# Spatial gating finished in two rounds, expert matrices stored by tile, and the last rows fetched right behind the last adds, in an encoder layer on one Trainium2 core

## The chip, the core and the metric

The kernel runs on 1 core of one Trainium2 chip. The metric is the device time of one execution in microseconds (us); smaller is better. The engines are TensorE (PE, matrix products), VectorE (DVE), ScalarE (ACT), GpSimd (POOL, which also issues the indirect DMAs) and SyncE (SP, which issues all other DMAs).

## What is computed

One layer (T = 2048 tokens, D = 1024) in float32: an input projection to q, k, v, u and vs (512 columns each), neighbourhood attention on q, k, v, spatial gating on u and vs, an output projection with a layer norm, and a mixture of 16 SwiGLU experts (width 256) of which each token takes two of one group, with a second layer norm. What matters here, cut from the reference:

```python
def spatial_gating(u, vs, ln_g, ln_b, w_s, b_s):          # u, vs after gelu
    vg = vs.reshape(B, T, 8, 64)
    vg = layer_norm(vg, ln_g.reshape(8, 64), ln_b.reshape(8, 64))
    vg = vg.reshape(B, n_chunks, 128, 8, 64)
    mixed = jnp.einsum('gpq,bnqgd->bnpgd', w_s, vg) + jnp.transpose(b_s)[:, :, None]
    return u * mixed.reshape(B, T, 512)

for e in range(16):
    act = jax.nn.silu(hf @ w_gate[e]) * (hf @ w_up[e])
    y = y + combine[:, e:e + 1] * (act @ w_down[e])
x = layer_norm(DEEPNORM_ALPHA * x + y, ln2_g, ln2_b)
```

## The kernel before

Each float32 product is made of three passes: both operands are split into a high part (a cast on ACT, line 142) and a low part (a subtraction on DVE, line 143), and PE adds high by high, low by high and high by low (lines 132 to 134).

*Phase A* is the input projection. The tokens go in two halves; `block(h, col, ...)` multiplies half `h` by column group `col` (0 q, 1 k, 2 v, 3 u, 4 vs) in two sets of four units, each in 8 k-steps. The order is (0,2), (0,4), (0,1), (0,3), (0,0), (1,0), (1,4), (1,3), (1,1). What follows a set is a generator (`fin_vs` for column group 4, `fin_k` for 1, `fin_u` for 3): after each k-step's matmuls the `Pipe` runs every live generator up to its next `yield`, and the order in which they issue is the order on every engine. For each set of column group 4 `fin_vs` takes a gelu and sums (lines 246, 247), subtracts the means and squares piece by piece (lines 251, 254, 255), raises the variance to −1/2 on POOL (line 259), multiplies (line 265), applies gain `gb` and offset `bb` on POOL (lines 267, 268), splits into `vh` and `vl`, and multiplies by the 8 position matrices `wsh`, `wsl` into PSUM tile `mx` (2 buffers). The result plus the bias `bs` goes to tile `mt` (lines 288, 290) and from there to DRAM (`md`, line 294), where `fin_u` fetches it. `mt` has one buffer; `fin_k` uses the same room for two of the four pieces that it stores to `kd` (line 343, function `rooms`).

*The experts* are jobs j = 0 to 17, each with four quarters u = 0 to 3 (gate and up of two column tiles; `gate_up`), then `down(j)`, one job later. `load_gu` (lines 1058, 1060) fetches one 1024 x 128 matrix tile from `w_gate` or `w_up`, and `load_d` (line 1082) half a down matrix; each is split on ACT and DVE unless the job is 17. `gather` (line 1112) brings token rows, `flip` (line 1131) transposes them, the scaled result `y` (line 1206) is added to `xad` in DRAM by an indirect DMA (line 1227). All indirect DMAs stand in POOL's queue.

The tokens are in four groups of experts. When a group's experts are done, `combine` fetches each tile of its rows (`fetch`, line 1449), waits `WAIT` steps, normalises it (`stats` on DVE, lines 1423, 1425; POOL, lines 1426, 1431; `first` and `second` on DVE, lines 1435, 1438) and stores it (`place`, line 1456). From job 15 on `CT` says at which quarters the next tile starts. The last group is done by `last`, whose table `TAIL` sets the order: `f` fetch, `s` statistics on DVE, `a` statistics on ACT (`act_stats`, lines 1473 to 1479), `c` and `v` the two DVE passes, `d` the last expert's product added to a fetched row (lines 1195, 1495), `o` store. The first entry of the table is issued at job 17, quarter 2.

Of the kernel before, what the change touches and what calls it, by code (L numbers as in the profile page):

```python
# [17 lines left out]
P = 128  # L18
# [22 lines left out]
NVT = 12  # L41
PSTART = 21
LATE = 14
YA = 3
YB = 2
YG = 0
FIRST = 256
WARM = 8
# [11 lines left out]
D32 = (17,)  # L60
DN = 0, 0
TU = 3
CT = (0, 2)
TAIL = "f0 f3 f1 f4 f2", "s0 c0 d3 a1 v0 d4 o0 c1 a2 v1 o1 c2 a3 v2 o2 a4 c3 v3 o3 c4 v4 o4"
AW1 = 3
AW2 = 4
LW = (1, 2), (2, 1)
# [78 lines left out]
def phase_a(c, xT, w_in, wsT, bsT, sg_g, sg_b):  # L146
# [8 lines left out]
    with ExitStack() as es:  # L155
# [54 lines left out]
        def load_sgu():  # L210
            nt, ng = 3 * E * S // P, 8 * T // P
            z = sp.tile([P, nt + ng], I32, name="mt")
            zt, zg = z[:, 0:nt].rearrange("p (r o) -> p r o", o=3), z[:, nt:].rearrange("p (r o) -> p r o", o=2)
            nc.vector.memset(z, 0)
            for v in (zt, zg):
                nc.vector.memset(v[:, :, 1:2], NONE)
            nc.vector.memset(zg[:, :, 0:1], T)
            nc.sync.dma_start(c.table[:, :].rearrange("(p c) o -> p c o", p=P), zt)
            nc.sync.dma_start(c.gtok[:, :].rearrange("(p c) o -> p c o", p=P), zg)
            nc.sync.dma_start(gb, bcast(sg_g, 512))  # L220
            nc.sync.dma_start(bb, bcast(sg_b, 512))
            nc.sync.dma_start(bs, bsT)
            wsr = sp.tile([P, 8, P], F32, name="mt")
            nc.sync.dma_start(wsr, wsT)
            yield
            yield
            split(nc, wsh[:, :, :], wsl[:, :, :], wsr[:, :, :])
            yield pipe

        def fin_v(h, units, ps):  # L230
# [10 lines left out]
        def fin_vs(h, units, ps):  # L241
            q = (h * 8 + units[0]) // 4
            g = [ev.tile([P, 8, 64], F32, name="g", bufs=8) for _ in range(4)]
            su = ev.tile([P, 4, 8], F32, name="su")
            for n in range(4):
                nc.scalar.activation(g[n], ps[n], AF.Gelu_apprx_tanh)
                nc.vector.tensor_reduce(su[:, n], g[n], axis=AX.X, op=OP.add)
            yield
            va = ev.tile([P, 4, 8], F32, name="va")
            for n in range(4):  # L250
                nc.vector.scalar_tensor_tensor(g[n], su[:, n, :, None].to_broadcast([P, 8, 64]), -1.0 / 64, g[n],
                                               op0=OP.mult, op1=OP.add)
                sq = ev.tile([P, 8, 64], F32, name="sq")
                nc.scalar.activation(sq, g[n], AF.Square)
                nc.vector.tensor_reduce(va[:, n], sq, axis=AX.X, op=OP.add)
            nc.vector.tensor_scalar(va, va, 1.0 / 64, EPS, op0=OP.mult, op1=OP.add)  # L256
            yield
            r = ev.tile([P, 4, 8], F32, name="r")
            nc.gpsimd.tensor_tensor(r, va, mhalf[:, :, :], op=OP.pow)  # L259
            yield  # L260
            yield
            vh = sp.tile([P, 4, 512], F32R, name="vh")
            vl = sp.tile([P, 4, 512], F32R, name="vl")
            for n in range(4):
                nc.vector.tensor_tensor(g[n], g[n], r[:, n, :, None].to_broadcast([P, 8, 64]), op=OP.mult)
                f = g[n][:, :, :].rearrange("p a d -> p (a d)")
                nc.gpsimd.tensor_tensor(f, f, gb, op=OP.mult)
                nc.gpsimd.tensor_tensor(f, f, bb, op=OP.add)
                yield
            for _ in range(YA):  # L270
                yield
            for n in range(4):
                f = g[n][:, :, :].rearrange("p a d -> p (a d)")
                split(nc, vh[:, n, :], vl[:, n, :], f)
            for _ in range(YB):
                yield
            mt = sp.tile([P, 4, 512], F32, name="mt")
            for g2 in range(4):
                pm = mx.tile([P, 2, 4, 64], F32, name="mx")
                for j in range(2):  # L280
                    e = g2 * 2 + j
                    s = slice(e * 64, (e + 1) * 64)
                    passes(nc, pm[:, j], wsh[:, e, :], wsl[:, e, :], vh[:, :, s], vl[:, :, s], True, True)
                for j in range(2):
                    e = g2 * 2 + j
                    s = slice(e * 64, (e + 1) * 64)
                    if j:
                        nc.vector.tensor_scalar(mt[:, :, s], pm[:, j], bs[:, e:e + 1], None, op0=OP.add)
                    else:
                        nc.scalar.activation(mt[:, :, s], pm[:, j], AF.Identity, bias=bs[:, e:e + 1])  # L290
                if g2 % 2 or YG:
                    yield
            for n in range(4):
                nc.sync.dma_start(md[q * 4 + n], mt[:, n, :])
            yield pipe
# [688 lines left out]
class Moe:  # L984
# [56 lines left out]
    def load_gu(self, pipe, j, f, lag=1):  # L1041
# [7 lines left out]
            r = self.raw()[:, :].rearrange("p (k f) -> p k f", k=KC)  # L1049
            l = self.wp.tile([P, KC, P], F32R, name="wl")  # L1050
        m, q = divmod(f, 2)
        s = slice(m * P, (m + 1) * P)
        e = bass.ds(self.ex[pos], 1)
        if lo:
            r4 = r.rearrange("p (k o) f -> p k o f", o=2)
            for i in range(2):
                src = self.w[i][e, q * 512:(q + 1) * 512, s]
                nc.sync.dma_start(r4[:, :, i], src.rearrange("o (k p) f -> (o p) k f", p=P))
        else:
            self.issued = nc.sync.dma_start(r, self.w[q][e, :, s].rearrange("o (k p) f -> (o p) k f", p=P)).ins.name  # L1060
        self.gw[j, f] = (r, None) if whole else (h, l)
        if whole:
            return
# [222 lines left out]
    def main(self):  # L1286
# [150 lines left out]
        def second(z, r):  # L1437
            V.scalar_tensor_tensor(z, z, r, lnb[0:z.shape[0], :], op0=OP.mult, op1=OP.add)

        def norm(x):  # L1440
            mean, r = stats(x)
            first(x, x, mean, OP.subtract)
            yield
            second(x, r)
            yield
# [12 lines left out]
            tc.declare_no_dep(r.ins, group=group, reason="rows of other tokens")  # L1458
            tc.add_to_no_dep_group(group, r.ins)

        def combine(g, rec):
            x = fetch(g, rec)
            for _ in range(WAIT):
                yield
            yield from norm(x)
            place(x, rec)
            yield pipe

# [78 lines left out]
        def over(mi, i):  # L1547
# [5 lines left out]
            for q, w in enumerate((w_gate, w_up)):  # L1553
                t = self.xp[0].tile([P, KC, W], F32R, name=("xh", "xl")[q])
                f = t[:, :, 0:FF].bitcast(F32)
                nc.sync.dma_start(f, w[bass.ds(e, 1)].rearrange("o (k p) f -> (o p) k f", p=P))
                wts.append(f)
            wd = self.xp[1].tile([P, 2, D], F32, name="xh")
            nc.sync.dma_start(wd, w_down[bass.ds(e, 1)].rearrange("o (k p) d -> (o p) k d", p=P))
# [37 lines left out]
        for j in range(2, nj):  # L1597
# [4 lines left out]
            for u in range(4):  # L1602
# [24 lines left out]
                if j < nj - 1 and j - 1 in LASTS and u == (TU if j == nj - 4 else 3):  # L1627
                    todo += [(LASTS[j - 1], i) for i in range(GTILES[LASTS[j - 1]])]
                pipe.step()
                if todo and u in (CU if j < nj - 3 else CT):  # L1630
                    g, i = todo.pop(0)
                    pipe.add(combine(g, recs[g][:, i]))
                if j == nj - 1 and u >= 2:
                    if u == 2:
                        tail = last(GTILES[3])
                    else:
                        pipe.flush()
                        assert not todo
                    next(tail)
# [40 lines left out]
    return mid.transpose(1, 0, 2), edge  # L1680


# [32 lines left out]
```

## Time and profile before

| | |
|---|---|
| median of 3 runs | 1328.71 us (1328.42 to 1332.13) |
| the profiled execution | 1326.6 us |
| its span in the trace | 1324.9 us |
| PE busy | 1230.7 us, 93% of the span |
| DVE, ACT, POOL busy | 59%, 43%, 34% |
| mean granted clock of PE | 0.972 |
| moved by DMA | 261.73 MB, mean 198 GB/s |

The span is the time from the first to the last recorded instruction; the execution's own time is 1.7 us longer. PE's share of busy time is an average over stages with different limits, so the share alone does not say what a change in one stage is worth. The granted clock is the share of TensorE's full speed that the chip gave.

### The profile page before, as it was taken

How to read it: one execution, taken by the hardware profiler on the slowest of the kernel's cores; microseconds unless marked ns; L12 is line 12 of the kernel's file. 1: busy time of each engine (PE TensorE's matmuls, PEld its weight loads, DVE VectorE, ACT ScalarE, POOL GpSimd, SP SyncE). 2: the span in 40 equal slices, each digit the busy share in tenths (PEclk: the TensorE clock that was granted, in tenths of full speed). 3: DMA queues.
4: the chain of work that ended last, by engine and by line, in shares of the span. 5: the costliest groups of instructions: out<-in, count | busy, mean ns of one | idle time of the engine just before them, and what ended most of it. 6: DMA issues, size and time to landing. Idle time of an engine off the chain costs nothing. (4 is left out here: it accounts for less than half of the span.)

```text
span 1324.9 us, 22205 instructions
## 1 busy us (share of the span) xinstructions
PE 1230.7 (93%) x7932; PEld 1048.7 (79%) x7932; DVE 775.6 (59%) x1622; ACT 576.1 (43%) x1218; POOL 452.4 (34%) x448
## 2 busy tenths in 40 slices
PE   9998999999899997999999999988888999998980
PEld 7886888888788775888888888768777999998970
DVE  5358233424853226576676676876466568777655
ACT  5324233322342236545545445334466555555522
POOL 0046000003710013234435434442323357565475
PEclk9998999999899997999999999999999999999995
DMA  8602634450254689578668676372999999999984
GB/s 253 199 24 97 229 120 164 161 189 18 89 182 167 180 257 289 170 187 199 166 187 196 160 219 194 97 227 76 257 277 301 250 270 287 297 293 306 280 250 137
DMA packets 193506, 261.73 MB, mean 198 GB/s; under 512 B 51120, under 2 KB 126128, under 8 KB 193392
## 3 DMA queue, kind: packets, MB, share of 16 engines
q1 hardware_dynamic: 175408, 204.88, 51.6%
q0 software_dynamic: 17984, 55.40, 14.9%
q8 instruction: 63, 1.03, 0.3%
q14 instruction: 51, 0.42, 0.1%
HBM read 184.17 MB, written 80.24 MB: 200 GB/s over the span
## 5 line engine op out<-in xcount | busy, mean ns | idle before, releaser
L143 DVE TENSOR_TENSOR wl<-wr,wh 128x512 fp32r<-128x512 f32 (+1 forms) x132 | 139.4, 1063 | 96.8 <-ACT wh L142 95.6
L618 POOL TENSOR_SCALAR lg<-lg,s 128x352 f32<-128x352 f32 (+3 forms) x128 | 80.2, 626 | 289.6 <-DVE s L617 226.4
L142 ACT CAST wh<-wr 128x512 fp32r<-128x512 f32 (+1 forms) x132 | 109.6, 843 | 85.0 <-DMA wr<-w_in 41.1
L132 PE MATMUL acc<-wh,xh 128*128 128x512 f32 x320 | 125.9, 393 | 0.1
L133 PE MATMUL acc<-wl,xh 128*128 128x512 f32 x320 | 125.3, 392 | 0.2 <-DVE wl L143 0.2
L134 PE MATMUL acc<-wh,xl 128*128 128x512 f32 x320 | 125.3, 391 | 0.2
L132 PE MATMUL gu<-xh,wh 128*128 128x256 f32 (+2 forms) x416 | 124.5, 299 | 0.0
L134 PE MATMUL gu<-xh,wl 128*128 128x256 f32 (+2 forms) x416 | 124.0, 298 | 0.0
L133 PE MATMUL gu<-xl,wh 128*128 128x256 f32 (+2 forms) x416 | 123.9, 298 | 0.0
L132 PE MATMUL acc<-xh,wh 128*128 128x512 f32 x256 | 101.0, 395 | 0.7 <-DVE kt L143 0.7
L134 PE MATMUL acc<-xh,wl 128*128 128x512 f32 x256 | 100.3, 392 | 0.0
L133 PE MATMUL acc<-xl,wh 128*128 128x512 f32 x256 | 100.2, 391 | 0.0
L633 ACT COPY pT<-pt 128x384 f32<-128x384 f32 (+3 forms) x128 | 57.7, 451 | 97.4 <-PE pt L631 95.3
L605 DVE CUSTOM_DVE_ANT_0 lg<-l,tm 128x352 f32<-128x352 f32 (+3 forms) x128 | 57.8, 452 | 70.6 <-PE l L134 45.2
L259 POOL TENSOR_TENSOR r<-va,mhalf 128x32 f32<-128x32 f32 x4 | 22.5, 5636 | 212.3 <-DVE va L256 212.3
L1227 POOL DMA_INDIRECT xad<-y,ix x38 | 64.7, 1704 | 54.4 <-ACT y L1206 31.6
L1112 POOL DMA_INDIRECT xg<-x1d,ix x40 | 48.1, 1203 | 101.8 <-PE tp L1131 37.0
L132 PEld LDWEIGHTS gu<-xh,wh 128*128 128x128 f32 x416 | 79.5, 191 | 1.4
L133 PEld LDWEIGHTS gu<-xl,wh 128*128 128x128 f32 x416 | 79.2, 190 | 1.3
L134 PEld LDWEIGHTS gu<-xh,wl 128*128 128x128 f32 x416 | 79.1, 190 | 0.0
L134 PEld LDWEIGHTS acc<-wh,xl 128*128 128x128 f32 x320 | 60.3, 189 | 13.7 <-DVE xl L143 1.1
L133 PEld LDWEIGHTS acc<-wl,xh 128*128 128x128 f32 x320 | 60.4, 189 | 13.2 <-DVE wl L143 0.9
(325 smaller groups left out, 3230.2 us busy)
## 6 DMA issues: line engine op xcount, KB each, us to landing
wr<-w_in SPq DMA_DIRECT2D x72, 256.0 KB
wr<-w_down SPq DMA_DIRECT2D x34, 512.0 KB
kt<-kd SPq DMA_DIRECT2D x24, 704.0 KB
wr<-w_gate SPq DMA_DIRECT2D x30, 512.0 KB
wr<-w_up SPq DMA_DIRECT2D x30, 512.0 KB
sd<-kt SPq DMA_DIRECT2D x16, 512.0 KB
qb<-qd SPq DMA_DIRECT2D x64, 128.0 KB
sr<-sd SPq DMA_DIRECT2D x16, 512.0 KB
```

The lines of the kernel that those rows point to most:

```text
L132: nc.tensor.matmul(out, lhsT=ahi, rhs=bhi, start=first, stop=False)
L133: nc.tensor.matmul(out, lhsT=ahi, rhs=blo, start=False, stop=False)
L134: nc.tensor.matmul(out, lhsT=alo, rhs=bhi, start=False, stop=last)
L142: nc.scalar.copy(hi, src)
L143: nc.vector.tensor_tensor(lo, src, hi.bitcast(F32), op=OP.subtract)
L259: nc.gpsimd.tensor_tensor(r, va, mhalf[:, :, :], op=OP.pow)
L605: nc.vector.tensor_tensor_reduce(out=l[:, :N], in0=o.rearrange("p r c -> p (r c)"), in1=bias, scale=-1.0, scalar=3.0e38, op0=OP.add, op1=O ...
L618: nc.gpsimd.tensor_scalar(l[:, :N], l[:, :N], s, 1.0, op0=OP.mult, op1=OP.mult)
L633: nc.scalar.copy(w[0:n, 0:len(ch)], pt[0:n, 0:len(ch)])
L1112: nc.gpsimd.indirect_dma_start(out=self.xg[(self.slot[j] + s) % NXG][0:m, :], out_offset=None, in_=c.x1d[0:rows, :], in_offset=bass.Indire ...
L1227: return self.c.nc.gpsimd.indirect_dma_start(out=self.c.xad[0:rows, :], out_offset=bass.IndirectOffsetOnAxis(ap=ix, axis=0), in_=y, in_off ...
```

## The change

- *Gating.* In `fin_vs` the loop that subtracts and squares becomes two loops; the power is raised in the same step; the gain is applied on DVE before the power is needed; the offset goes out of the loop. Since the position product is linear, the offset's part of it is the row sum of each position matrix times the offset, which is computed once in `load_sgu` (8 one-column products, then `bb` becomes offset times row sum plus bias) and added by one DVE instruction per two matrices. All four pieces are split in one step, and the products come `YB` = 4 steps later (`YA` goes).
- *By tile.* `by_tile` lays `w_gate` and `w_up` out in memory, on the host, so that each 1024 x 128 tile has for each partition one run of 1024 floats (4 KB) where it had 8 runs of 128 (512 B).
- *The end.* Of the five tiles of group 2 (g = 2) the first starts at (14,3) as before, the others at (15,0), (15,1), (15,3) and (16,0) in place of (15,0), (15,2), (16,0) and (16,2); their statistics are taken on ACT, and one step sooner after the fetch. The first entry of `TAIL` is issued at quarter 1 of job 17, in the order f0 to f4; `TAIL` has no `s`.

```diff
@@ constants
-YA = 3
-YB = 2
+YB = 4
-CT = (0, 2)
-TAIL = "f0 f3 f1 f4 f2", "s0 c0 d3 a1 v0 d4 o0 c1 a2 v1 o1 c2 a3 v2 o2 a4 c3 v3 o3 c4 v4 o4"
+CT = (0, 1, 3), (0,)
+TAIL = "f0 f1 f2 f3 f4", "a0", "a1 c0 v0 o0 a2 c1 v1 o1 d3 a3 c2 v2 o2 d4 a4 c3 v3 o3 c4 v4 o4"
@@ load_sgu
             split(nc, wsh[:, :, :], wsl[:, :, :], wsr[:, :, :])
+            for _ in range(8):
+                yield
+            pr = mx.tile([P, 8], F32, name="mx")
+            for e in range(8):
+                nc.tensor.matmul(pr[:, e:e + 1], lhsT=wsr[:, e], rhs=c.ones, start=True, stop=True)
+            rs = sp.tile([P, 8], F32, name="rs")
+            nc.vector.tensor_copy(rs, pr)
+            for e in range(8):
+                s = slice(e * 64, (e + 1) * 64)
+                nc.vector.tensor_scalar(bb[:, s], bb[:, s], rs[:, e:e + 1], bs[:, e:e + 1], op0=OP.mult, op1=OP.add)
@@ fin_vs
+            for n in range(4):
                 sq = ev.tile([P, 8, 64], F32, name="sq")
                 nc.scalar.activation(sq, g[n], AF.Square)
...
-            yield
             r = ev.tile([P, 4, 8], F32, name="r")
             nc.gpsimd.tensor_tensor(r, va, mhalf[:, :, :], op=OP.pow)
+            yield
+            for n in range(4):
+                f = g[n][:, :, :].rearrange("p a d -> p (a d)")
+                nc.vector.tensor_tensor(f, f, gb, op=OP.mult)
+            yield
...
                 nc.vector.tensor_tensor(g[n], g[n], r[:, n, :, None].to_broadcast([P, 8, 64]), op=OP.mult)
                 f = g[n][:, :, :].rearrange("p a d -> p (a d)")
-                nc.gpsimd.tensor_tensor(f, f, gb, op=OP.mult)
-                nc.gpsimd.tensor_tensor(f, f, bb, op=OP.add)
-                yield
-            for _ in range(YA):
-                yield
+                nc.scalar.copy(vh[:, n, :], f)
             for n in range(4):
                 f = g[n][:, :, :].rearrange("p a d -> p (a d)")
-                split(nc, vh[:, n, :], vl[:, n, :], f)
+                nc.vector.tensor_tensor(vl[:, n, :], f, vh[:, n, :].bitcast(F32), op=OP.subtract)
...
-                for j in range(2):
-                    e = g2 * 2 + j
-                    s = slice(e * 64, (e + 1) * 64)
-                    if j:
-                        nc.vector.tensor_scalar(mt[:, :, s], pm[:, j], bs[:, e:e + 1], None, op0=OP.add)
-                    else:
-                        nc.scalar.activation(mt[:, :, s], pm[:, j], AF.Identity, bias=bs[:, e:e + 1])
+                s = slice(g2 * 128, g2 * 128 + 128)
+                add = bb[:, s].rearrange("p (j d) -> p j d", j=2)[:, :, None, :].to_broadcast([P, 2, 4, 64])
+                nc.vector.tensor_tensor(mt[:, :, s].rearrange("p n (j d) -> p j n d", j=2), pm, add, op=OP.add)
@@ load_gu
-            self.issued = nc.sync.dma_start(r, self.w[q][e, :, s].rearrange("o (k p) f -> (o p) k f", p=P)).ins.name
+            self.issued = nc.sync.dma_start(r, self.w[q][e, m].rearrange("o p k f -> (o p) k f")).ins.name
@@ norm, combine
-        def norm(x):
-            mean, r = stats(x)
-            first(x, x, mean, OP.subtract)
+        def norm(x, late=False):
+            mean, r = act_stats(x) if late else stats(x)
+            first(x, x, mean, OP.add if late else OP.subtract)
...
-            for _ in range(WAIT):
+            for _ in range(WAIT - late):
                 yield
-            yield from norm(x)
+            yield from norm(x, late)
@@ run
-                if todo and u in (CU if j < nj - 3 else CT):
+                if todo and u in (CU if j < nj - 3 else CT[j - nj + 3]):
                     g, i = todo.pop(0)
-                    pipe.add(combine(g, recs[g][:, i]))
-                if j == nj - 1 and u >= 2:
-                    if u == 2:
+                    pipe.add(combine(g, recs[g][:, i], g == 2))
+                if j == nj - 1 and u >= 1:
+                    if u == 1:
                         tail = last(GTILES[3])
-                    else:
+                    if u == 3:
                         pipe.flush()
@@ host
+def by_tile(w):
+    return w.reshape(E, KC, P, 2, P).transpose(0, 3, 2, 1, 4)
```

How the order moves on three engines. First ACT from the first set of block (0,4) on (`sq` the squares, `vh` the high part for the products, `wh` weights of the next blocks, `g` the gelu). Before:

```order
L246 ACTIVATE g<-acc 128x512 x4
L254 ACTIVATE sq<-g 128x512 x4
L142 CAST wh<-wr 128x512 x4
L246 ACTIVATE g<-acc 128x512 x4
L254 ACTIVATE sq<-g 128x512 x4
L142 CAST vh<-g 128x512 x4
L142 CAST wh<-wr 128x512
L290 ACTIVATE mt<-mx,bs 128x4x64 x2
```

and now:

```order
L255 ACTIVATE g<-acc 128x512 x4
L264 ACTIVATE sq<-g 128x512 x4
L141 CAST wh<-wr 128x512
L281 CAST vh<-g 128x512 x4
L141 CAST wh<-wr 128x512 x3
L255 ACTIVATE g<-acc 128x512 x4
L264 ACTIVATE sq<-g 128x512 x4
L141 CAST wh<-wr 128x512
L281 CAST vh<-g 128x512 x4
```

The first set's `vh` stood behind the second set's gelu and squares; now it stands ahead of that gelu, and the additions to `mt` are gone from ACT.

ACT in the last experts, from the activation of quarter (15,2) on (`wh`, `dh` weights, `a` the product's high part, `xh` transposed rows, `y` the scaled result). Before:

```order
L1177 ACTIVATE sg<-gu 128x256
L142 CAST wh<-wr 128x1024
L142 CAST a_9502<-sg 128x256
L142 CAST wh<-wr 128x1024
L1177 ACTIVATE sg<-gu 128x256
L1133 COPY xh<-tp 128x4x128 x2
L1206 ACTIVATE y<-yp,ix 128x512 x2
```

and now:

```order
L1182 ACTIVATE sg<-gu 128x256
L1478 ACTIVATE junk,csu<-cx 128x1024
L1479 ACTIVATE csu<-csu 128x1
L1483 ACTIVATE junk,csu<-cx,csu 128x1024
L141 CAST wh<-wr 128x1024
L141 CAST a_9489<-sg 128x256
```

Three instructions on a fetched tile `cx` of group 2 come in between the activation and the weight cast; the same three follow behind the cast `a`, and three times more further on.

POOL from the adds of job 16 (`xad<-y`) to the last group's fetches (`cx<-xad` and `xg<-xad` fetches, `out<-cx` stores, `cmv`, `csu`, `cr` statistics). Before:

```order
L1227 DMA xad<-y,ix 2048x1024 x2
L1456 DMA out<-cx,crec 2048x1024
L1426 TENSOR_SCALAR cmv<-cmv 128x1
L1431 TENSOR_TENSOR cr<-cmv,mhalf 128x1
L1456 DMA out<-cx,crec 2048x1024
L1426 TENSOR_SCALAR cmv<-cmv 128x1
L1431 TENSOR_TENSOR cr<-cmv,mhalf 128x1
L1449 DMA cx<-xad,crec 128x1024
L1449 DMA xg_2_9067<-xad,ix 128x1024
L1449 DMA cx<-xad,crec 128x1024
L1449 DMA xg_0_9482<-xad,ix 64x1024
```

and now:

```order
L1232 DMA xad<-y,ix 2048x1024 x2
L1461 DMA out<-cx,crec 2048x1024 x2
L1454 DMA cx<-xad,crec 128x1024 x3
L1454 DMA xg_2_9054<-xad,ix 128x1024
L1454 DMA xg_0_9469<-xad,ix 64x1024
L1484 TENSOR_SCALAR csu<-csu 128x1
L1436 TENSOR_TENSOR cr<-csu,mhalf 128x1
```

The five fetches came behind two rounds of statistics and stores of group 2; now only two stores stand between the adds and the fetches, and they follow one another.

## Rows read from the trace of the kernel before

**Rows 1.** The page, part 1: busy time, share, instructions by engine.

```profile
PE 1230.7 (93%) x7932; PEld 1048.7 (79%) x7932; DVE 775.6 (59%) x1622; ACT 576.1 (43%) x1218; POOL 452.4 (34%) x448
```

**Rows 2.** Windows around the mixing products: busy time by engine, clock, DMA share, GB/s.

```profile
104.00:107.50 3.50, 3.50 (x17) 2.73 (x15) 1.98 (x4) 1.27 (x2) 0.00 (x0) 1.00 0.00 0
107.50:117.80 10.30, 5.82 (x19) 4.78 (x19) 6.03 (x12) 4.69 (x9) 6.67 (x2) 0.67 0.01 2
343.60:353.30 9.70, 5.57 (x19) 4.68 (x19) 5.44 (x11) 4.68 (x9) 6.44 (x2) 0.65 0.00 0
```

**Rows 3.** PE timeline there: start, duration, instruction [idle before <- releaser].

```profile
111.43 0.58 PE L132 MATMUL mx<-vh,wsh 128*128 128x256 f32 x1 [3.73 <-ACT vh L142]
112.76 0.58 PE L133 MATMUL mx<-vl,wsh 128*128 128x256 f32 x1 [0.74 <-DVE vl L143]
...
128.35 0.50 PE L132 MATMUL acc<-xh,wh 128*128 128x512 f32 x1 [0.73 <-DVE kt L143]
```

**Rows 4.** ACT timeline, the same stage.

```profile
106.63 0.63 ACT L254 ACTIVATE sq<-g 128x512 f32<-128x512 f32 x1 [1.41 <-DVE g L251]
```

**Rows 5.** DVE timeline: a weight split beside POOL work, and one without.

```profile
97.60 1.78 DVE L143 TENSOR_TENSOR wl<-wr,wh 128x512 fp32r<-128x512 f32 x1
...
143.42 0.69 DVE L143 TENSOR_TENSOR wl<-wr,wh 128x512 fp32r<-128x512 f32 x1
```

**Rows 6.** POOL timeline, the same stage.

```profile
97.20 1.62 POOL L268 TENSOR_TENSOR g<-g,bb 128x512 f32<-128x512 f32 x1
```

**Rows 7.** Groups of PE by line: count, busy us, mean ns, idle before.

```profile
L881 PE MATMUL l<-ones,sq 128*128 128x1 f32 x32 | 4.7, 252 | 0.0
```

**Rows 8.** SyncE timeline (DMA issues) at the end of a k-set.

```profile
129.71 2.15 SPq L343 DMA_DIRECT2D kd<-mt  x2
```

**Rows 9.** Windows: the start of the experts, and two near the end.

```profile
925.00:1040.00 115.00, 99.85 (x652) 90.54 (x651) 68.27 (x102) 65.35 (x102) 34.58 (x27) 0.99 0.96 272
1245.00:1250.00 5.00, 5.00 (x44) 5.00 (x44) 3.32 (x5) 1.62 (x3) 3.18 (x2) 1.00 1.06 277
1270.00:1275.00 5.00, 5.00 (x22) 4.07 (x23) 1.65 (x2) 2.20 (x4) 4.34 (x5) 1.00 1.03 354
```

**Rows 10.** SyncE timeline, L1060: first and last of 17 loads.

```profile
926.85 0.38 SPq L1060 DMA_DIRECT2D wr<-w_gate  x1
...
1039.31 0.37 SPq L1060 DMA_DIRECT2D wr<-w_gate  x1
```

**Rows 11.** POOL timeline: a fetch of group 2, the last group's first.

```profile
1242.12 1.05 POOL L1449 DMA_INDIRECT cx<-xad,crec  x1 [0.30 <-issue]
...
1287.67 1.64 POOL L1449 DMA_INDIRECT cx<-xad,crec  x1 [0.66 <-issue]
```

**Rows 12.** DVE timeline: first statistics of group 2.

```profile
1252.00 1.29 DVE L1423 BATCH_NORM_STATS2 cst<-cx 128x6 f32<-128x512 f32 x2 [3.21 <-DMA cx<-xad,crec]
```

**Rows 13.** ACT timeline: two casts of experts, two passes of the tail.

```profile
1245.13 1.08 ACT L142 CAST wh<-wr 128x1024 fp32r<-128x1024 f32 x1
1247.93 0.41 ACT L142 CAST a<-sg 128x256 fp32r<-128x256 f32 x1 [1.72 <-DVE sg L1180]
...
1298.53 1.06 ACT L1473 ACTIVATE junk<-cx 128x1024 f32<-128x1024 f32 x1 [17.93 <-DMA cx<-xad,crec]
...
1301.22 1.06 ACT L1473 ACTIVATE junk<-cx 128x1024 f32<-128x1024 f32 x1
```

**Rows 14.** Window behind the longest wait of the last 100 us.

```profile
1214.00:1217.50 3.50, 3.50 (x19) 3.30 (x17) 3.50 (x5) 1.95 (x4) 2.63 (x2) 0.59 1.03 374
```

**Rows 15.** PE waits, 1200 to 1300 us: total, times, longest.

```profile
PE yp L132 <- ACT a L142: 4.9, 2, 3.9
PE gu L1195 <- DVE sg L1180: 2.9, 1, 2.9
```

**Rows 16.** PE timeline: a down product, and the last products.

```profile
1250.41 0.48 PE L132 MATMUL yp<-dh,a 128*128 128x512 f32 x1
...
1286.64 6.42 PE L1195 MATMUL gu<-dh,sg 128*128 128x512 f32 x14 [2.95 <-DVE sg L1180]
```

More of the change, by code (lines that the diff above doesn't have):

```diff
@@ L1051, in load_gu @@
         m, q = divmod(f, 2)
-        s = slice(m * P, (m + 1) * P)
         e = bass.ds(self.ex[pos], 1)
@@ L1056, in load_gu @@
             for i in range(2):
-                src = self.w[i][e, q * 512:(q + 1) * 512, s]
-                nc.sync.dma_start(r4[:, :, i], src.rearrange("o (k p) f -> (o p) k f", p=P))
+                src = self.w[i][e, m, :, q * 4:(q + 1) * 4, :]
+                nc.sync.dma_start(r4[:, :, i], src.rearrange("o p k f -> (o p) k f"))
         else:
-            self.issued = nc.sync.dma_start(r, self.w[q][e, :, s].rearrange("o (k p) f -> (o p) k f", p=P)).ins.name
+            self.issued = nc.sync.dma_start(r, self.w[q][e, m].rearrange("o p k f -> (o p) k f")).ins.name
         self.gw[j, f] = (r, None) if whole else (h, l)
@@ L1459, in place, with combine @@
             tc.add_to_no_dep_group(group, r.ins)
-        def combine(g, rec):
+        def combine(g, rec, late):
             x = fetch(g, rec)
-            for _ in range(WAIT):
+            for _ in range(WAIT - late):
                 yield
-            yield from norm(x)
+            yield from norm(x, late)
             place(x, rec)
@@ L1555, in over @@
                 f = t[:, :, 0:FF].bitcast(F32)
-                nc.sync.dma_start(f, w[bass.ds(e, 1)].rearrange("o (k p) f -> (o p) k f", p=P))
+                for m in range(2):
+                    src = w[bass.ds(e, 1), m].rearrange("o p k f -> (o p) k f")
+                    nc.sync.dma_start(f[:, :, m * P:(m + 1) * P], src)
                 wts.append(f)
@@ L1700 @@
         b_r=np.concatenate([i["router_group_b"][0], i["router_expert_b"][0]]),
-        w_gate=i["expert_w_gate"][0], w_up=i["expert_w_up"][0], w_down=i["expert_w_down"][0],
+        w_gate=by_tile(i["expert_w_gate"][0]), w_up=by_tile(i["expert_w_up"][0]), w_down=i["expert_w_down"][0],
         ln2g=i["ln2_g"][0], ln2b=i["ln2_b"][0],
```

## The prediction

> **What bounds the kernel now.** I read the page first: TensorE (PE) is busy 93% of the span [rows 1], so a change pays only where PE waits, or after its last product. Then I read PE's waits stage by stage, and the timelines of the engines that it waits for. Three places matter.
>
> *Gating.* In two stretches, one in each half of the sequence, PE stops in front of the position-mixing products for 3.73 us and then 0.74 us, for the casts `vh` (ACT) and `vl` (DVE) [rows 3], and comes back at about half clock: the two windows of 10.3 and 9.7 us have 5.82 and 5.57 us of matmuls at a mean clock of 0.67 and 0.65, against 1.00 before [rows 2]: 2.4 GHz for a part and 1.2 GHz for the rest. The casts are late because ACT stands between two squares for 1.41 us, waiting for DVE's subtraction [rows 4], and DVE subtracts the next piece only after it has summed ACT's square: the engines alternate, four pieces long, ahead of the casts in both queues. POOL multiplies and adds beside them [rows 6], and while it does, a DVE subtraction of one shape takes 1.78 instead of 0.69 us [rows 5].
>
> *Start of the experts.* From 925 to 1040 us PE is busy 99.85 of 115 us, with the DMA engines at a share of 0.96 [rows 9]: 15.2 us idle, much of it behind weights.
>
> *The end.* PE has its last product at 1293 us [rows 16], after waits of 4.9 and 2.9 us in the last 100 [rows 15]. Then the last rows have to be fetched, normalised and stored: POOL issues the first of their five fetches only at 1287.67 [rows 11], and the program ends over 30 us behind PE.
>
> **The sum, step by step**, against the profiled execution (1326.6 us, which is 2.1 below the median of the runs).
>
> *Gating, removed.* Idle 10.3 − 5.82 = 4.5 us, and clock lost 0.33 × 10.3 = 3.4 us: 7.9 at most. The second stretch gives 4.1 + 3.4 = 7.5. Idle time inside the slow part (the 0.74 us) is counted twice in this, so 7.5 and 7.1. With all subtractions ahead of the squares the alternation ends; casts come five k-steps after the set and products four later, so they have some 6 us to spare. POOL's two passes go, so the wait of 0.73 us behind `kt` [rows 3] should go too. Sum −15.3. Four more multiplications per set on DVE, 0.69 us each [rows 5], lie in time where DVE waits for POOL or ACT; without that cover they would push `vl` back by 2.8 us, within the 6.
>
> *Gating, added.* Eight one-column products for the row sums. The same shape takes 0.25 us each elsewhere [rows 7], 4.7 us for 32: 1.2 to 2.0 us on PE, I take +1.5. Then a new wait: the second set's results go to tile `mt`, which has one buffer and which the k-set just finished also uses for two of its four stores. Before, the products came four steps later. The two of `mt` were issued from 129.71 us [rows 8], 2.1 us behind the end of that set's matmuls (128.35 − 0.73 [rows 3]); with 2 MB of such stores at 354 GB/s at best [rows 9] the buffer is free some 6 to 10 us behind the end. PE has two PSUM buffers, so half of the products and a k-step of matmuls as cover: 24 instructions at 3.5 / 17 = 0.21 us [rows 2], 4.9 us. With what each later buffer adds, it waits 0 to 6 us; DVE's queue (weight splits for the next block) stands behind it. I take +1, for DVE is no longer slowed and casts faster than in the row.
>
> *Expert matrices by tile.* Gate and up matrices are read in runs of 4 KB instead of 512 B. At full DMA share, 5 us with many such loads moved 277 GB/s, 5 us without them 354 [rows 9]. A 512 KB load would go from 1.89 to 1.48 us. Seventeen of them are issued from 926.85 to 1039.31 [rows 10]: 17 × 0.41 = 7 us less transfer, of 15.2 us idle. Not all of that is for weights (transposes wait for gathered rows), and packets of POOL's queue compete. Between 0 and −10 I take −5. Later PE is busy throughout and it gives nothing by itself.
>
> The Trainium skill says otherwise (DMA: Bandwidth & Descriptors, Specifications): a transfer of 512 B or more already runs at line rate. By it this term is 0 and the sum 5 us higher. The two windows [rows 9] speak against it, though they also differ in what POOL's queue moves.
>
> *The last experts.* Group 2's rows are now normalised by ACT, one step earlier, in ACT's own queue ahead of casts that PE needs. The first fetch was issued at 1242.12 [rows 11] and landed at 1252.00, where DVE had waited 3.21 us for it [rows 12]. In the new order ACT would stand there instead, then need 2.69 us (two passes, the distance of the first two passes in the tail [rows 13]), before the `wh` cast that it did at 1245.13 and the cast `a` that it did at 1247.93 [rows 13]. DVE's first product step waits for the same statistics ahead of its `wl` and `sg`. 1252.0 + 2.7 + some 2.5 for `wh`, `sg` and `a` is 1257; PE's product of `a` began at 1250.41 [rows 16]. So a new stall of up to 6 us, about 4 if transfers are faster. The fourth and fifth fetches put two more (5 and 3 us by the same reckoning) ahead of the next expert's `a`. Against that go the 2.9 us [rows 15] and 1.0 of the 4.9 (the other 3.9 is group 1's and stays), and four us behind PE: the five fetches come as one run right behind the adds, and the first two tiles are finished under products, so DVE has two pairs of passes instead of four behind the last product, but five statistics of 2.69 us on ACT take the place as bound. Best: −4 − 4 = −8, no new stall. Worst: −8 + 14 + 3 for half clock behind long stalls (as behind the 3.9 us one: 0.59 in the next 3.5 us [rows 14]) = +9. I take +4, nearer to the worst, because the landing times are measured ones.
>
> Sum: −15.3 + 1.5 + 1 − 5 + 4 = −13.8. From 1326.6 that is 1312.8; from the median of the runs, 1314.9. I predict **1315 us**.
>
> **Rivals.**
> - *The end works.* Faster transfers bring group 2's rows in time (DVE waited only 3.21 us at the first), ACT has time (busy 1.62 of 5 us [rows 9]), and the tail gives its −8 in place of +4: 1303. For it speaks ACT's load; against it the 10 us from issue to landing.
> - *By tile brings nothing:* the loads are bound by something else than the run length: 1315 + 5 = 1320. It is what the rule of the Trainium skill above would give.
> - *The room.* The wait for `mt` is 6 us with half clock behind it (3.4), instead of 1: 1315 + 8.4 = 1323. It decides if the stores land later than 9 us behind the set.
> - *It doesn't do what it says.* The casts still come late, since DVE now has the multiplications too; one stall of some 7.3 in each half remains: 1330, no change.
> - *Slower.* ACT stands behind each of the five fetches, and each stall delays the outputs whose add is queued ahead of the next fetch on POOL, so the next lands later too. One costs 9.9 (issue to landing) + 2.7 − 3.0 (lead over the cast) − 2.5 (from the cast `a` to its product [rows 13, 16]) = 7 us; five are 35. Without the tail's term the time is 1311; + 35 − 8 = 1338. It decides against the change once these stalls pass some 26 us in all (1311 − 8 + 26 = 1329).
>
> **How the numbers follow.** A measurement of this kernel tells about 0.3% (4 us) from no change: faster is below 1324.7. Chances: forecast 0.50, end works 0.20, by tile nothing 0.14, room 0.07, not what it says 0.03, slower 0.06. The first three are faster (0.84), and the room is on the border: I count it and the next one as no change (0.10); slower 0.06. The range leaves out the slower case and most of the border ones: 1299 (end works, by tile −9) to 1325.
>
> **What would show it.** Right: no `vh` wait ahead of the mixing products, clock 1.00 there, POOL with only the power; less PE idle than 15.2 us from the experts' start to the same place; ACT waiting for `cx` rows of group 2, and PE for `a`. Wrong: PE behind `mx` or DVE behind `mt` in the second set of the k-block; 512 B loads no faster; no wait of ACT for `cx`, and PE's last product more than 15 us earlier than at 1293 (then the end works); or PE idle above 20 us in the last two experts (slower).

## The result and the profile after

The changed kernel takes 1322.43 us (median of 6 runs, 1318.39 to 1325.34) against 1330.49 us of the kernel before measured beside it (6 runs, 1328.42 to 1334.15): a ratio of 0.9936, 95% interval 0.9913 to 0.9959. That is 8.5 us faster (5.5 to 11.6), where 13.8 were forecast. The profiled execution took 1322.18 us, with a span of 1320.5.

A few marks of the traces say where the time went; that of the kernel before is of an execution of 1326.6 us, faster than all six timed beside the changed kernel, so the marks show 4.4 us and not 8.5. "Attention" is the start of the first attention product, behind both halves of the gating; "down (15,0)" the first down product of job 15; "last product" the end of PE's last one. The differences are against the kernel before.

| | attention | down (15,0) | last product | end of the span |
|---|---|---|---|---|
| before | 447.8 | 1250.4 | 1293.1 | 1324.9 |
| changed | 432.8 (−15.0) | 1233.0 (−17.4) | 1291.5 (−1.6) | 1320.5 (−4.4) |

So the changed kernel gained 15 us up to the gating's end, another 2.4 up to job 15, and then the last two jobs lost 15.8 of these 17.4; 2.8 came back behind the last product.

*Gating.* Windows of the changed kernel's timeline in both halves (columns as in [rows 2]):

```profile
95.00:105.00 10.00, 10.00 (x57) 8.72 (x56) 7.77 (x13) 3.89 (x7) 0.00 (x0) 1.00 0.04 15
120.00:127.00 7.00, 6.95 (x37) 5.63 (x35) 1.41 (x3) 1.45 (x4) 0.00 (x0) 1.00 0.84 314
127.00:135.00 8.00, 7.09 (x37) 6.12 (x38) 4.57 (x7) 1.00 (x2) 0.00 (x0) 1.00 0.47 163
340.00:365.00 25.00, 25.00 (x125) 21.11 (x124) 14.24 (x26) 10.01 (x21) 1.01 (x1) 1.00 0.48 163
```

The clock is 1.00 in all of them, where [rows 2] had 0.67 and 0.65, PE is busy throughout but for 0.9 us from 127 us on, and in these windows POOL is all but idle (outside them it has one power of 5.4 to 5.9 us per set). The one wait that is left is the new one that was forecast, for the room. PE's and DVE's timelines there:

```profile
127.91 0.39 PE L131 MATMUL mx<-vh,wsh 128*128 128x256 f32 x1 [0.95 <-DVE mt L296]
```

```profile
120.03 1.37 DVE L142 TENSOR_TENSOR mt<-acc,mt 128x512 fp32r<-128x512 f32 x2
127.16 1.29 DVE L296 TENSOR_TENSOR mt<-mx,bb 128x512 f32<-128x512 f32 x2 [5.75 <-DMA kd<-mt]
```

DVE is done with the pieces for `kd` at 121.4 and stands until 127.16 for the stores that read `mt`; PE, with two PSUM buffers as cover, loses 0.95 us. The row sums took 1.84 us on PE (16 matmuls from 44.48 us on).

*The last two jobs.* ACT's timeline of the changed kernel, from the activation of (15,2) on:

```profile
1227.84 0.41 ACT L1182 ACTIVATE sg<-gu 128x256 f32<-128x256 f32 x1
1233.85 1.06 ACT L1478 ACTIVATE junk<-cx 128x1024 f32<-128x1024 f32 x1 [5.60 <-DMA cx<-xad,crec]
...
1236.41 1.03 ACT L141 CAST wh<-wr 128x1024 fp32r<-128x1024 f32 x1
1239.33 0.41 ACT L141 CAST a<-sg 128x256 fp32r<-128x256 f32 x1 [1.89 <-DVE sg L1185]
...
1261.21 1.06 ACT L1478 ACTIVATE junk<-cx 128x1024 f32<-128x1024 f32 x1 [4.67 <-DMA cx<-xad,crec]
...
1265.55 0.40 ACT L141 CAST a<-sg 128x256 fp32r<-128x256 f32 x1 [1.69 <-DVE sg L1185]
```

ACT comes to the first rows of group 2 at 1228.2 and stands 5.60 us until they land. The weight cast, DVE's split and the cast `a` follow only then; before, the two casts were at 1245.13 and 1247.93 [rows 13]. The product that needs this `a` is the fourth down product of (15,0): the first three ran without a wait, from 1232.97 us in the changed kernel. Before, the fourth ran in its turn:

```profile
1251.19 0.39 PE L132 MATMUL yp<-dh,a 128*128 128x512 f32 x1
```

The fourth tile of group 2 makes ACT wait again, until 1261.21. PE's timeline of the changed kernel shows the price:

```profile
1239.79 0.80 PE L131 MATMUL yp<-dh,a 128*128 128x512 f32 x1 [5.87 <-ACT a L141]
...
1266.01 0.80 PE L131 MATMUL yp<-dh,a 128*128 128x512 f32 x1 [6.13 <-ACT a L141]
...
1272.14 0.80 PE L131 MATMUL yp<-dh,a 128*128 128x512 f32 x1 [1.93 <-ACT y L1211]
```

These are 13.9 us, and PE comes back at half clock (1.2 GHz) each time. Windows behind the three waits, the third line just ahead of the third wait:

```profile
1239.80:1243.30 3.50, 3.50 (x8) 2.81 (x9) 1.59 (x2) 2.18 (x4) 0.85 (x1) 0.50 0.52 172
1266.00:1269.50 3.50, 3.49 (x8) 2.84 (x9) 1.61 (x2) 0.86 (x1) 0.00 (x0) 0.50 0.66 268
1269.50:1270.20 0.70, 0.70 (x2) 0.00 (x0) 0.00 (x0) 0.64 (x4) 0.00 (x0) 0.50 0.40 164
1272.20:1276.50 4.30, 4.30 (x13) 3.40 (x14) 1.70 (x2) 1.16 (x2) 3.54 (x3) 0.63 0.00 0
```

The waits of [rows 15] are gone: 3.9 us and 1.0 of ACT's `a`, and 2.9 of `sg`.

*Transfers.* The page's part 3 (packets, MB, share of 16 engines), of the kernel before and then of the changed one:

```profile
q1 hardware_dynamic: 175408, 204.88, 51.6%
q0 software_dynamic: 17984, 55.40, 14.9%
```

```profile
q1 hardware_dynamic: 118064, 204.88, 49.7%
q0 software_dynamic: 17984, 55.40, 15.4%
```

Queue 1 has 118,064 packets for the same 204.88 MB, where it had 175,408, and 49.7% of 1320.5 us on each engine instead of 51.6% of 1324.9: 27 us less. POOL's queue, with the same 17,984 packets, takes 6 us more (15.4% against 14.9%). All fourteen traces agree: the four with the old layout have 684 to 689 us in queue 1 and 196 to 198 in POOL's, the ten by tile 656 to 663 and 202 to 206.

### The profile page after: what moved, and what is told of

Same layout as the page of the kernel before. It is cut to its first block, busy times and chain, and to the rows that moved or that the text cites. A ratio compares the mean times of both kernels' runs of the same rounds, so it can differ in the third digit from the quotient of the medians.

```text
span 1320.5 us, 22228 instructions
## 1 busy us (share of the span) xinstructions
PE 1233.7 (93%) x7948; PEld 1052.7 (80%) x7948; DVE 755.7 (57%) x1629; ACT 585.8 (44%) x1232; POOL 405.7 (31%) x416
## 3 DMA queue, kind: packets, MB, share of 16 engines
q1 hardware_dynamic: 118064, 204.88, 49.7%
q0 software_dynamic: 17984, 55.40, 15.4%
## 5 line engine op out<-in xcount | busy, mean ns | idle before, releaser
L142 DVE TENSOR_TENSOR wl<-wr,wh 128x512 fp32r<-128x512 f32 (+1 forms) x132 | 125.6, 964 | 100.8 <-ACT wh L141 100.1
L131 PE MATMUL yp<-dh,a 128*128 128x512 f32 (+1 forms) x136 | 59.5, 437 | 19.2 <-ACT a L141 17.3
```

What stands on the lines that cost most here:

```text
L131: nc.tensor.matmul(out, lhsT=ahi, rhs=bhi, start=first, stop=False)
L142: nc.vector.tensor_tensor(lo, src, hi.bitcast(F32), op=OP.subtract)
```

## The experiments

Each run stands beside runs of the kernel before on the same chip; ratios are to those. Attention, down (15,0), last product and end are read as above.

| run | time | ratio (95%) | attention | down (15,0) | last product | end |
|---|---|---|---|---|---|---|
| gating alone | 1317.45 | 0.9879 (0.9839 to 0.9919) | 433.4 | 1249.2 | 1292.9 | 1322.0 |
| by tile alone | 1323.88 | 0.9963 (0.9942 to 0.9983) | 448.1 | 1246.4 | 1290.7 | 1321.6 |
| end alone | 1344.88 | 1.0112 (1.0075 to 1.0149) | 447.5 | 1251.6 | 1305.6 | 1335.1 |
| changed, statistics on DVE | 1306.71 | 0.9822 (0.9789 to 0.9855) | 433.9 | 1235.3 | 1277.1 | 1305.0 |
| changed, ACT, three steps | 1305.62 | 0.9796 (0.9765 to 0.9828) | 433.6 | 1230.7 | 1276.0 | 1304.0 |
| gating and by tile | 1306.48 | 0.9805 (0.9773 to 0.9838) | 433.5 | 1234.2 | 1278.1 | 1307.2 |
| DVE, old quarters | 1308.16 | 0.9818 (0.9786 to 0.9849) | 433.3 | 1235.8 | 1280.5 | 1310.1 |
| parted loop alone | 1315.73 | 0.9886 (0.9842 to 0.9929) | 434.6 | 1239.2 | 1283.1 | 1314.2 |
| DVE, loop joined again | 1310.94 | 0.9860 (0.9833 to 0.9887) | 439.7 | 1239.1 | 1281.9 | 1310.0 |
| parted loop and by tile | 1309.28 | 0.9857 (0.9829 to 0.9885) | 435.1 | 1234.1 | 1277.1 | 1307.4 |
| ACT, three steps, room first | 1312.42 | 0.9857 (0.9817 to 0.9898) | 432.3 | 1232.5 | 1278.2 | 1305.8 |

### The three parts, each alone

*Gating alone* (the edits of `load_sgu` and `fin_vs`, and `YB`).

> The kernel before with the gating part alone. In the changed kernel the attention stage stands 13.9 us earlier than before. My theory: the parts add up, this one gives those 14 us and nothing downstream takes them back: about 1316, ratio 0.9895. Rival: the later stages are bound by transfers that do not start earlier, so a part of it is given back and it ends above 1321 (ratio over 0.993).

Measured: 1317.45, ratio 0.9879, so 12 us faster by the medians and 16 by the ratio. Attention begins 14.4 us earlier, as forecast. The six runs spread from 1306.2 to 1331.8, so the total is not exact; the stage is. The profiled execution, 1323.69, is one of the slower ones, and at (15,0) only 1.2 of its 14.4 us are left. Much of that went in one place, where ACT waited for an up tile and PE behind it:

```profile
1019.80 1.04 ACT L141 CAST wh<-wr 128x1024 fp32r<-128x1024 f32 x1 [9.44 <-DMA wr<-w_up]
```

```profile
1022.76 0.48 PE L1169 MATMUL tp<-ident,sg 128*128 128x128 f32 x1 [8.39 <-DVE xl L142]
```

So the rival, that transfers give a part back, holds for this execution, though not for the median.

*By tile alone* (`by_tile` and the loads).

> The kernel before with gate and up matrices by tile alone. My theory: longer runs make the loads shorter; in the changed kernel the experts up to 1230 us gained 3.5 us in all, so 1327 (ratio 0.9975), and windows with many loads move more than 277 GB/s at full share. Rival, the rule that 512 B are at line rate: within 1 us of before and the same GB/s at full share.

Measured: ratio 0.9963, 4.9 us faster (2.3 to 7.7): the rival of no gain is out. But the gain is not where the prediction put it. From 927 to 1042 us PE is busy 99.15 of 115 us, no better than before (99.85 [rows 9], and 99.85 in the same window). ACT's timeline in that stage, by tile and then before:

```profile
946.83 1.26 ACT L1205 ACTIVATE y<-o,ix 128x512 f32<-128x512 f32 x2 [5.36 <-DMA xad<-y,ix]
```

```profile
943.29 1.27 ACT L1206 ACTIVATE y<-o,ix 128x512 f32<-128x512 f32 x2 [3.01 <-DMA xad<-y,ix]
```

The `y` behind a transfer of POOL's queue (an add into `xad`, issued at 937.40 and at 936.84 us) waits 5.36 us instead of 3.01: the add lands 9.4 us after its issue instead of 6.5. Other traces agree: by tile (changed, gating and by tile, parted loop and by tile) this wait is 4.7 to 5.5 us, with the old layout 2.2 in the run with gating alone and none with the parted loop alone. PE's next transposes wait behind this for 5.9 us instead of 3.5, and PE's busy time in the stage did not grow. The gain comes later, where the prediction had given nothing, in front of the stall of 3.9 us [rows 15]. SyncE's issue of one gate tile, and ACT's cast of it, before:

```profile
1181.45 0.37 SPq L1060 DMA_DIRECT2D wr<-w_gate  x1
```

```profile
1195.70 1.05 ACT L142 CAST wh<-wr 128x1024 fp32r<-128x1024 f32 x1 [3.64 <-DMA wr<-w_gate]
```

and by tile:

```profile
1181.73 0.33 SPq L1059 DMA_DIRECT2D wr<-w_gate  x1
```

```profile
1193.30 1.04 ACT L142 CAST wh<-wr 128x1024 fp32r<-128x1024 f32 x1
```

The load that was issued at 1181.45 landed at 1195.70 and kept ACT 3.64 us; by tile, ACT does not wait for it. DVE's queue then runs 4 us earlier against PE (the product `sg` comes 12.3 instead of 16.2 us behind the same down product), and the stall of 3.9 us with its half clock [rows 14] is gone: from that down product to the one of (15,0) it takes 50.2 us (1196.2 to 1246.4) instead of 55.6 (1194.8 to 1250.4). In all four traces with the old layout ACT waits for this gate tile (2.7 to 3.6 us) and PE stalls behind it (3.0 to 3.9 us); in none of the ten by tile does PE stall there. DVE's passes for group 1 stand ahead of `sg` in both; the late tile made the difference. By tile, a tile is also one contiguous piece of DRAM; the runs do not part this from the length of the packets.

*The end alone* (`CT`, `TAIL`, `late`, the place of `last`).

> The kernel before with the end part alone. My theory: ACT stands in its queue for the rows of group 2 ahead of casts that PE needs, so PE waits some 14 us more in the last two experts than before, 4 of which come back behind PE: 9 to 13 us slower, 1339 to 1343 (ratio 1.007 to 1.010). Rival: the loss in the changed kernel came from the other parts, which moved the end against the transfers; then this one is no slower than before (ratio at most 1.000).

Measured: ratio 1.0112, 14.9 us slower (10 to 20), so the loss is the part's own. PE's waits from 1190 us on:

```profile
PE yp L132 <- ACT a L142: 13.6, 3, 5.9
```

The first of the three, 3.1 us at 1213, is the stall that the kernel before has too; the end's own are 5.9 and 4.6. The profiled execution, 1336.93, is the fastest of the six, so its marks show 10.2 us.

Product of the three ratios: 0.9879 × 0.9963 × 1.0112 = 0.9953, against 0.9936 (0.9913 to 0.9959) for all three: within these intervals the parts add up.

### Which edit of the end costs

*Statistics on DVE again*, all else as changed:

```diff
-                    pipe.add(combine(g, recs[g][:, i], g == 2))
+                    pipe.add(combine(g, recs[g][:, i], False))
```

> The changed kernel with the statistics of group 2 on DVE again, three steps behind the fetch; order and places of the fetches stay. My theory: the waits of PE for the cast a (17.3 us in all) fall below 6 us and the time to about 1310 (ratio 0.985 against before). Rival: it is the place of the fetches and adds on POOL, or DVE's queue, that makes PE late; then PE still waits over 12 us there and the time stays at 1320 to 1323 (ratio 0.992 to 0.995).

Measured: 1306.71, ratio 0.9822; PE's waits in the last jobs are one of 1.8 us. That is 3 us better than my theory's number, but the edit undid two things at once, the engine and the step.

*On ACT, three steps behind the fetch:*

```diff
-            for _ in range(WAIT - late):
+            for _ in range(WAIT):
```

> The changed kernel with group 2's statistics still on ACT, but three steps behind the fetch as before. It parts the two things that the change did: the engine and the step. My theory: both count; the rows then land before or soon after ACT gets there (they landed 5.6 us after ACT came to them in the changed kernel, and a step is about 3 us), so PE's waits in the last two experts fall from 14 to some 6 us: 1312 to 1316 (ratio 0.987 to 0.990). Rival: the engine alone counts (ACT's two passes lie ahead of the casts in any case): over 10 us of waits, 1320. Other rival: the step alone counts: 1307.

Measured: 1305.62, ratio 0.9796: the second rival's number. By the times, the step costs all of it and the engine nothing that can be told. ACT's timeline shows why:

```profile
1228.36 0.41 ACT L141 CAST a<-sg 128x256 fp32r<-128x256 f32 x1 [1.73 <-DVE sg L1185]
1232.21 1.06 ACT L1478 ACTIVATE junk<-cx 128x1024 f32<-128x1024 f32 x1 [3.45 <-DMA cx<-xad,crec]
...
1234.78 1.03 ACT L141 CAST wh<-wr 128x1024 fp32r<-128x1024 f32 x1
...
1239.31 1.06 ACT L1478 ACTIVATE junk<-cx 128x1024 f32<-128x1024 f32 x1 [1.09 <-DMA cx<-xad,crec]
```

The cast `a` now stands ahead of the statistics. ACT still waits 3.45 us for the rows, but what PE needs next has been issued. One wait of PE is left, in job 16's down products:

```profile
1254.48 0.50 PE L131 MATMUL yp<-dh,a 128*128 128x512 f32 x1 [4.71 <-ACT a L141]
```

My theory had held that both count, and the marks bear it out in part. From (15,0) to the last product it took 58.5 us in the changed kernel, 45.3 here (45.3 and 45.8 in the two runs below that are made from this one), 41.8 with the statistics on DVE (42.8 with the loop joined again). So the step is worth some 13 us and the engine some 3. The times do not show these 3 us: the profiled execution here came to (15,0) 4.6 us earlier than that with DVE, behind jobs in which the two kernels are the same. Statistics on DVE with the early step were not run, so whether the step would cost as much there stays open.

*Without any of the end part* (gating and by tile on the kernel before):

> The changed kernel without its whole end part: gating and by tile on the kernel before. My theory: the parts add up, 0.988 x 0.996 = 0.984, 1308 to 1310; the run with statistics on DVE (1306.7) is then 2 to 3 us better by the early fetch of the last group. Rival: the early fetch gives nothing, as the stores at the end wait for the same passes: equal to that run within 1 us.

Measured: 1306.48, ratio 0.9805: the rival's number. Neither the early fetch nor ACT's statistics bring anything that these runs can tell; the changed kernel's end part costs some 16 us (1322.4 against 1306.5; 17 by the ratios), and its best form gives none.

*DVE, old quarters* (`CT = (0, 2), (0, 2)`):

> The run with statistics on DVE, and group 2's tiles started at the quarters of before. My theory: what is left of the end part is the early fetch of the last group, and the places of group 2's fetches matter little: within 2 us of 1306.7. Rival: starting the tiles later puts the last of them behind the last group's fetches, and the end comes over 4 us later.

Measured: 1308.16, ratio 0.9818: as my theory had it.

### What in the gating part gives the gain

*The loop parted*, one edit in the kernel before:

```diff
                                                op0=OP.mult, op1=OP.add)
+            for n in range(4):
                 sq = ev.tile([P, 8, 64], F32, name="sq")
```

> The kernel before with one edit: the loop that subtracts and squares is parted in two, nothing else of the gating part. My theory of the cause: DVE and ACT alternate four times at 2.04 us ahead of the casts; with two loops they need 4 x 0.69 + 0.6 + 4 x 0.69 = 6 instead of 8.2 us, so the wait of 3.73 us falls to some 1.5 and the clock does not fall: about 9 us in the two halves, 1320 (ratio 0.993). Rival: the casts are late because POOL's passes slow DVE and because the first set's casts stand behind the second set's gelu at all; then the wait stays over 2.5 us with half clock and the gain is under 4 us.

Measured (4 runs): ratio 0.9886, 15.2 us faster, more than expected. ACT's timeline there:

```profile
101.69 1.23 ACT L255 ACTIVATE sq<-g 128x512 f32<-128x512 f32 x2 [1.11 <-DVE va L256]
102.82 2.17 ACT L142 CAST vh<-g 128x512 fp32r<-128x512 f32 x4
```

The casts `vh` begin at 102.82 instead of 109.21 us, and PE's waits up to 420 us are one of 1.6 us for `kt` and small ones; none for `vh` or `vl`. Attention begins 13.2 us earlier, of 14.4 with the whole gating part. The casts gain 6.4 us where I had reckoned 2.2, since the loop stands ahead of them twice: parted in the first set, it brings the second set's sums on DVE 3.2 us forward, and in the second set it gives 3.2 us more. DVE's timeline, before and then with the loop parted:

```profile
99.30 2.45 DVE L247 TENSOR_REDUCE su<-g 128x8 f32<-128x512 f32 x4
```

```profile
96.10 2.45 DVE L247 TENSOR_REDUCE su<-g 128x8 f32<-128x512 f32 x4
```

So parting the loop is enough. POOL's passes are still there and a DVE instruction beside them still takes 1.78 us, so they did not have to go; that they added nothing to the delay is not shown, as no run took them alone away.

*The loop joined again*, in the run with statistics on DVE:

> The run with statistics on DVE, with subtraction and square in one loop again; all else of the gating part stays. Parting the loop alone gave the whole gain (the attention stage began 13.2 us earlier, of 14.4 with the whole part). My theory now: either of the two is enough, since with the casts of the first set ahead of the second set's gelu the alternation is off PE's path: no wait for vh, the attention stage at 434 us, time within 3 us of 1306.7. Rival: the alternation is the cause wherever it stands, and the waits come back: 1318 or more.

Measured: 1310.94, ratio 0.9860, between the two. There is no wait for `vh`, though the engines alternate as before, so the other edits of the gating part are enough for that as well. But attention begins at 439.7, 5.8 us later. DVE and PE in the second set of block (0,1):

```profile
122.48 1.29 DVE L142 TENSOR_TENSOR mt<-acc,mt 128x512 fp32r<-128x512 f32 x2
130.68 1.29 DVE L295 TENSOR_TENSOR mt<-mx,bb 128x512 f32<-128x512 f32 x2 [6.91 <-DMA kd<-mt]
```

```profile
131.42 0.58 PE L131 MATMUL mx<-vh,wsh 128*128 128x256 f32 x1 [3.57 <-DVE mt L295]
```

DVE's pieces for the room are 2.5 us later than in the changed kernel (122.48 against 120.03), DVE can write the room at 130.68 instead of 127.16, and PE's wait grows from 0.95 to 3.57 us. The rival "room" of the prediction is real; 2.5 us on DVE decided it here.

*Parted loop and by tile, nothing else:*

> The kernel before with two edits only: the subtract-and-square loop parted, and the matrices by tile. My theory: these are all of the gain; the attention stage begins at 434.6 as with the parted loop alone, and the rest runs as in the run without the end part: 1307 to 1309 (ratio 0.982). Rival: the whole gating part is worth more than the parted loop (POOL freed, ACT relieved): above 1311.

Measured: 1309.28, ratio 0.9857, span 1307.4 against 1307.2 of the run with the whole gating part. By the medians, one line and the new layout give all but 2.8 us of that run's gain; by the ratios, each with its own runs of before, all but 0.005 (7 us), with intervals that overlap. Whether the rest of the gating part gives anything stays open.

### Two more

*Another order of the last group* (`TAIL = "f3 f0 f4 f1 f2", "", "d3 a0 d4 a3 c0 v0 o0 a4 a1 c3 v3 o3 c4 v4 o4 a2 c1 v1 o1 c2 v2 o2"`). The step is that of the run with ACT and three steps. In this order the stores `o1` and `o2` come behind those of the last expert's rows, and part of the last rows lacks that expert's share.

> Statistics on ACT three steps behind the fetch (1305.6), and the last group in another order: the two rows of the last expert first, f3 f0 f4 f1 f2, their products added while the other fetches land, and the passes packed so that DVE never stands. DVE stood 7.9 us for the first rows and had 15.5 us of passes behind that. My theory: the end is bound by DVE's passes behind the first landing, and the two additions (3 us) move ahead of it: 1302 to 1303 (ratio 0.977). Rival: the end is bound by ACT's three statistics of 2.7 us or by the last store's wait: 1305 to 1306.

Measured: 1312.45, ratio 0.9872: slower than the run it was made from by some 7 us (10 by the ratios). From the last product to the end it took 31.8 us against 28.0, so about 4 us are the order's own. The expectation was wrong; nothing was gained.

*The room's pieces stored first* (`rooms(False)` in `fin_k`, in the run with ACT and three steps):

> The run with ACT's statistics three steps behind the fetch (1305.6), and in the first half the pieces that share a room with the mixing results are stored first of the four instead of last. With the alternation put back, PE waited 3.6 us for that room; in the changed kernel 0.95 us, and DVE 5.75 us. My theory: the room's stores are issued some 2 us earlier, DVE's wait falls to about 4 us and PE's 0.95 us goes: the attention stage begins 1 us earlier (432.5), 1304 to 1305. Rival: the stores land together anyway, as all four share the queues: DVE's wait and PE's stay within 0.5 us, no change.

In the stage it is as my theory had it. DVE's timeline:

```profile
119.05 1.37 DVE L142 TENSOR_TENSOR mt<-acc,mt 128x512 fp32r<-128x512 f32 x2 [0.95 <-ACT mt L141]
...
124.66 1.29 DVE L296 TENSOR_TENSOR mt<-mx,bb 128x512 f32<-128x512 f32 x2 [2.88 <-PE mx L133]
```

The pieces for `mt` are first, DVE waits 2.88 us for PE's products and no longer for a DMA, PE has no wait, and attention begins at 432.3 (433.6 without the edit). The time, 1312.42, does not show it: its six runs spread from 1304 to 1315 and those of before beside it from 1324 to 1339. Whether the 1.3 us reach the end stays open.

## Why the prediction was right, and where not

The side and the range were right (1299 to 1325); the size was 8.5 instead of 13.8 us. That 1322 lies within the range is in part luck: its upper bound stood for the room, and the end at its worst, +9, would have given 1320; the end was worse than that. By its own steps:

1. *Gating: −15.3 + 1.5 + 1 = −12.8.* Right: −15.0 in the changed kernel and −14.4 alone, with the row sums at 1.84 and the wait for the room at 0.95. That the alternation of DVE and ACT made the casts late was shown by the parted loop alone (−13.2); the joined loop shows that the other edits take the wait for `vh` away as well. What POOL's slowing of DVE [rows 5] added to it was not measured by itself.
2. *By tile: −5.* The size was right (4.9 alone), but by luck, for its place was wrong. The transfer saved per load, forecast as 0.41 us from two windows, shows in queue 1: 20 to 27 us less on each engine (by tile alone 50.2% of 1321.6, changed 49.7% of 1320.5). The 57,344 packets fewer are those of 64 loads of 512 KB (128 x 7 each; the 16 loads of 256 KB keep theirs), so 0.32 to 0.43 us each: the forecast was right in this. "Later PE is busy throughout and it gives nothing by itself" was the wrong sentence, with "the other 3.9 is group 1's and stays": that stall began with a late gate tile. At the experts' start PE gained nothing, and the later adds of POOL's queue, whose competition was named as a doubt, stood in the way.
3. *The rule of the Trainium skill* (DMA: Bandwidth & Descriptors, Specifications), 512 B at line rate, by which this term was 0: the runs disagree, 1323.9 against 1329.4 us, and queue 1 moved the same bytes in 20 to 27 us less on each engine.
4. *The end: +4.* This is the step that failed, a mis-sized term: it measured +14.9 alone and +13.0 in the changed kernel's marks (from −17.4 to −4.4). The new stalls had been reckoned at 6, 5 and 3 us and were 5.87, 6.13 and 1.93. The first agrees partly by luck: the fetch landed 7.6 us after its issue (1226.29 to 1233.85) and not 9.9, but it was issued 6.7 us ahead of (15,0) and not 8.3; and the product that needs the cast is the fourth, 0.8 us behind the one of [rows 16]. The half clock cost 5.8 us (15.8 + 3.95 − 13.9) instead of 3, since PE came back slow three times. The −4 for old waits came (3.95), and of the −4 behind the last product 2.8. By its own measured numbers the worst case was the likely one; I weakened it with "about 4 if transfers are faster" and took a value between.
5. *The rivals.* "The end works" was wrong for this change; with the statistics one step later the end is about harmless, but its gain did not come either. "By tile brings nothing" is out (2.3 to 7.7 us faster alone). The room cost 0.95 us and not 6. "Slower" named the right mechanism; the stalls with their clock came to 19.8 us, short of its 26.

## What to carry to other kernels

Where two engines hand pieces to and fro, issue all of the first's pieces ahead of the second's: one loop parted in two gave 15.2 us, more than the whole change as it was made (8.5). A wait for a slow transfer belongs in a queue behind whatever the bottleneck engine needs next; the same statistics on the same engine made a difference of some 16 us by one step. Cost a bundle of edits apart, and when measured landing times give the price of a new wait, take that price.

## What was not expected of the hardware

- With the weights in longer packets, an add into `xad` at the experts' start landed 9.4 us after its issue instead of 6.5, and POOL's packets, the same in number, took 4 to 10 us more of each engine in all (202 to 206 us against 196 to 198). Not all of that queue got slower: the median time from issue to landing, in the four traces that have it, is 8.9 to 9.3 us for the adds by tile (three) against 8.7 with the old layout (one), but 6.4 to 7.4 against 7.9 for the fetches `xg`.
- The third of the waits in the last two jobs was only 1.9 us long, but it came while PE was still at 1.2 GHz from the second; behind it the clock was 0.63 over 4.3 us. With three waits of 13.9 us in all went 5.8 us of clock.
